# Keeping two pairs of features on chip between gate/up and down, with store slots instead of a staging buffer

## The chip, the cores and the metric

The kernel runs on one core of one Trainium2 chip. Five engines work beside each other and wait for each other by semaphores: PE (matmuls into PSUM; the profile lists its weight loads as PEld), ACT and DVE (elementwise work, both reach PSUM and SBUF), POOL (elementwise work in SBUF) and SP, which here issues nearly all DMAs between HBM and SBUF. The metric is the device time of one execution in microseconds (us).

## What is computed

One layer of a hybrid decoder: three token mixers (dilated attention, a convolution module, sliding-window attention), an output projection with a residual, and a SwiGLU feed-forward block. There are 512 tokens, a model width of 2048 and a feed-forward width of 5632, all in float32. The change touches only the feed-forward block, the last two lines:

```python
def reference(x, norm1_g, w_in, ..., norm2_g, w_gate, w_up, w_down):
    for l in range(DEPTH):                      # DEPTH = 1
        h = _rms_norm(x, norm1_g[l])
        proj = h @ w_in[l]
        ...                                     # three mixers
        mix = jnp.concatenate([out_a, out_b, out_c], axis=-1)
        x = x + mix @ w_out[l]
        h2 = _rms_norm(x, norm2_g[l])
        x = x + (jax.nn.silu(h2 @ w_gate[l]) * (h2 @ w_up[l])) @ w_down[l]
    return x
```

## The kernel before

**Numbers and operands.** PE multiplies numbers of a shortened float32 form, so every operand is split into a high part (rounded) and a low part (what is left). A product is then high x high + high x low + low x high. Moving operands are tiles of 128 x 512: the left 256 columns hold the high part, the right 256 the low part of the same 256 tokens. A matmul with the weights' high part `wh` runs over all 512 columns, one with the low part `wl` over the left 256 and adds into the right half of the PSUM bank; the halves of the bank are added when DVE reads it out (`multiply`, L907 to L916).

**Seven products instead of eight.** The three matrix products of the feed-forward block are done on 2 x 2 blocks: output channels in halves, inputs in halves, tokens in halves. Seven products of sums of blocks, numbered 1 to 7 and taken in the order `ORDER` = 5, 1, 7, 6, 2, 4, 3, give all four output blocks. One such product is called a unit here, seven units a block of the loop at the end (L1071).

**Gate and up.** The 44 tiles of 128 features are taken as 22 pairs p = 0 to 21 (feature tiles p and p + 22). For each pair there is one block for gate and one for up (`Wide`), 44 blocks in all. Their moving operands are the 56 tiles `ops[q, j]` (7 products, 8 inputs j), which stay in SBUF until the last of these blocks. After the up block of a pair its two result tiles `l` and `r` are made into the seven operands that down needs, by POOL's sums `sums1` and `sums2` and by four calls of `piece` at fixed distances behind the block (`later(n, piece, ...)`). `piece` copies its source into PSUM in shortened form (`near`, ACT, L994), copies it again into the high columns of a staging tile (ACT, L995), subtracts to get the low columns (DVE, L996), and queues a store of the tile to the HBM tensor `od` of that pair. A staging tile has 1024 columns, that is two operands, and there are two of them. Three pieces hold two operands (512 KB), the last one holds one (256 KB). `LAID` says in which order the seven operands lie in `od`.

**Down.** 24 blocks (`Down`, `DOWN`) follow, in three rounds over 8 pairs of output tiles. Block t multiplies the operands of pairs `first` to `end - 1`: block d0 those of pairs 0 to 5, d1 0 to 6, d2 1 to 7, and so on with a window of seven that moves by one. Pairs 22 to 27 in this count are pairs 0 to 5 again, in the third round. `load_act(q, pairs)` loads operand q of the given pairs from `od` into slots. During the last gate/up block it is queued after each unit for pairs 0 to 5, 42 loads of 256 KB in all; during block t for the pairs that block t + 1 adds. Tiles with names `a` are these loaded operands.

**Weights.** Each block needs seven weight tiles: four come from HBM ('21', '22', '11', '12'), three are sums made by POOL ('s' in three states, '21' plus '11'; `group`, L160 to L185). `pump` (L204) lets SP issue the next weight loads when a raw buffer is free. `split_up_to` runs two units ahead: ACT makes `wn` in PSUM (L226) and `wh` in SBUF (L227), DVE makes `wl` (L228); three buffers each of `wh` and `wl`.

**Order of work and buffers.** Nothing reorders at run time: every engine goes through its instructions, and SP through its DMAs, in the order in which the program was written out, so a late instruction holds up all behind it on its engine. Work that is not to hold up the units is queued in `evacs` and `extras` and written out one unit at a time. SBUF tiles of 128 x 512 come from one pool of `N_SLOTS` = 71 slots; a tile is given the slot of an earlier one that is done, and its first writer waits for that tile's last reader.

Of the kernel before, what the change touches and what calls it, by code (L numbers as in the profile page):

```python
# [9 lines left out]
F32 = mybir.dt.float32  # L10
F32R = mybir.dt.float32r
# [4 lines left out]
P = 128  # L16
T = 512
# [26 lines left out]
        "bg3 ak2 cq4 ak0 av0 cq6 aq0 ak1 av1 aq1 av2 aq2 ak3 av3 aq3").split()  # L44
ROWS = "c0 c1 c2 c4 c5 c3 c7 c6 a0 a1 b2 b1 b0 b3 a2 a3".split()

N_SLOTS = 71

RAW_PLAIN = "22b sb 21 22a 11 sa 12".split()
RAW_BUFS = 7  # L50
# [12 lines left out]
TH = T // 2  # L63
NJ = KT // 2
NP = NF // 2


_A = [0, 0, 1, 2, 3, 4, 5, 6]
_B = [_A[n] + (6 if n == 0 else 7) for n in range(8)]
_C = [b + 8 for b in _B]  # L70
DOWN = [(n, *w) for ab in (zip(_A, _B), zip(_B, _C), zip(_C, [a + NP for a in _A])) for n, w in enumerate(ab)]

LAID = (5, 7, 6, 4, 3, 1, 2)
# [36 lines left out]
def kernel(ctx: ExitStack, tc: tile.TileContext, xT, wi, wo, wgu, wd, cst_in, outT):  # L110
    nc = tc.nc
    cp = ctx.enter_context(tc.tile_pool(name="consts", bufs=1))
    wp = ctx.enter_context(tc.tile_pool(name="weights", bufs=1))
    sp = ctx.enter_context(tc.tile_pool(name="slots", bufs=N_SLOTS))
    ctx.enter_context(tc.manual_schedule())
# [14 lines left out]
    def slot(name, dt=F32, cols=T):  # L130
        return sp.tile([P, cols], dt, name=name, tag="s")

    def bank(name, cols=T):
        return psum["banks"].tile([P, cols], F32, name=name, tag="b")
# [26 lines left out]
    def group(name, m, n, blocks):  # L161

        key = {k: (k, name) for k in ("11", "12", "21", "22", "s")}
        for k in ("21", "22", "11", "12"):
            entries.append((k + "ab"[m] if k == "22" else k, key[k], blocks[k]))
        u = len(works)

        def add(to, a, b, last=None):
            def go():
                if to == a:  # L170
                    out = raws[key[to]][0]
                else:
                    out = take("s" + "ab"[m], key[to], n)
                nc.gpsimd.tensor_add(out[:, :n], raws[key[a]][0][:, :n], raws[key[b]][0][:, :n])  # L174
                if last:
                    drop(key[last])
            return go

        sums[u - 4].append(add("s", "21", "22"))
        sums[u - 3].append(add("21", "21", "11"))  # L180
        sums[u].append(add("s", "s", "11", "11"))
        sums[u + 2].append(add("s", "s", "12"))
        works.extend((key[k], last, None) for k, last in (
            ("s", False), ("11", False), ("21", True), ("s", False), ("12", True), ("22", True), ("s", True)))

    for p in range(NP):
        for m in range(2):
            group(f"{'gu'[m]}{p}", m, 1024, {f"{i + 1}{k + 1}": [wgu[4 * (p + i * NP) + 2 * m + k]]
                                             for i in range(2) for k in range(2)})

    def down_block(n, half, first, end):

        parts = [(first, min(end, NP)), (0, end - NP)] if first < NP else [(first - NP, end - NP)]
        return [bass.AP(tensor=wd.tensor, offset=wd.offset + (n * P * NF + half * NP + a) * P,
                        ap=[[NF * P, P], [1, (b - a) * P]]) for a, b in parts if b > a]
# [6 lines left out]
    at = {"entry": 0, "split": 0, "use": 0}  # L202
# [29 lines left out]
    def sums_now():  # L232
        for fn in sums.pop(at["use"], ()):
            fn()

    def next_unit():
        sums_now()
        u = at["use"]
        at["use"] += 1
        split_up_to(u + SPLIT_AHEAD)  # L240
        pump(RAW_EARLY if u < 20 else RAW_BUFS)
        return splits.pop(u)
# [119 lines left out]
    for k in range(KT):  # L362
# [9 lines left out]
        hi, lo = h_hl.pop(k)  # L372
# [14 lines left out]
    def project(name):  # L387
        b = bank(name)
        for half in range(2):
            wh, wl = next_unit()  # L390
            for kk in range(8):
                k = 8 * half + kk
                s = slice(kk * P, (kk + 1) * P)
                mm3(b, wh[:, s], wl[:, s], h_hi[k], h_lo[k], k == 0, k == KT - 1)
                if kk % 2 == 1:
                    ticks.tick()
        return b
# [356 lines left out]
    for name in PROJ[HEAD4:]:  # L754
        kind, what, j = name[0], name[1], name[2:]
# [3 lines left out]
        b = project(name)  # L759
# [19 lines left out]
    b = box = boxes = shared = None  # L779
# [60 lines left out]
    for half in range(2):  # L840
        for i, n in enumerate(OUT_ORDER[half]):
            if half == 1 and i == 2:
                ticks.drain()
                b = None
                open_banks(banks=4, high=2)
            b = bank(f"o{half}_{n}")
            wh, wl = next_unit()
            for kk in range(8):
                k = 8 * half + kk
# [4 lines left out]
                s = slice(kk * P, (kk + 1) * P)  # L854
# [20 lines left out]
    def norm2a():  # L875
        n2["r"] = token_scale(ssum2, D, "n2", outs[3][:, :NT])[1]

    def norm2b():
        b = spread(n2["r"], "r2s", outs[3])
        nc.scalar.copy(R_12, b)  # L880
        nc.scalar.copy(r2b[:, T:], b[:, :TH])  # L881

    od = {p: tc.dram_tile([P, 7 * T], F32, name=f"od{p}") for p in range(NP)}
    evacs, extras = [], []
    flip = [1]

    def run(queue):

        for fn, *args in queue.pop(0) if queue else ():
            fn(*args)  # L890

    def later(n, fn, *args, queue=evacs):
        while len(queue) <= n:
            queue.append([])
        queue[n].append((fn, *args))
# [36 lines left out]
    class Wide(Block):  # L932
# [54 lines left out]

        def piece(self, at, src):
            n = src.shape[-1] // TH
            both = wp.tile([P, 2 * T], F32R, name=f"{self.name}st{at}", tag="stage", bufs=2)  # L990
            near = psum["high"].tile([P, 1024], F32R, name=f"{self.name}n{at}", tag="h")[:, :n * TH]
            hi, lo = (both[:, :n * T].rearrange("p (a b c) -> p a b c", a=n, b=2)[:, :, b] for b in range(2))
            src2, near2 = (t.rearrange("p (a b) -> p a b", a=n) for t in (src, near))
            nc.scalar.copy(near, src)  # L994
            nc.scalar.copy(hi, src2)  # L995
            nc.vector.tensor_sub(lo, src2, near2.bitcast(F32))  # L996
            later(0, nc.sync.dma_start, od[self.p][:, at * T:(at + n) * T], both[:, :n * T].bitcast(F32), queue=extras)

        def piece1(self):
            self.piece(0, self.ta)  # L1000
# [15 lines left out]
    def load_y(t):  # L1016
        if t < len(DOWN):
            for n in (DOWN[t][0], DOWN[t][0] + 8):
                y[t, n] = slot(f"y{t}_{n}")
                nc.sync.dma_start(y[t, n], x2d[n])  # L1020
# [37 lines left out]
                self.add(q, t[:, cols])  # L1058
                self.store(n, t, cols)

    acts = {}

    def load_act(q, pairs):
        for j in pairs:
            acts[q, j] = slot(f"a{q}_{j}", F32R)
            at = LAID.index(q)
            nc.sync.dma_start(acts[q, j].bitcast(F32), od[j % NP][:, at * T:(at + 1) * T])
# [3 lines left out]
    for g in range(2 * NP + len(DOWN)):  # L1071
        t = g - 2 * NP
        if t < 0:
            p, m = divmod(g, 2)
            blk = Wide(p, m, gate if m else None)
            gate = blk if m == 0 else None
        else:
            n, first, end = DOWN[t]
            blk = Down(t)
        early_w = []  # L1080
        for i, q in enumerate(ORDER):
            sums_now()
            run(evacs)
            w = next_unit()
            if g == 0 and i < 2:
                blk.multiply(q, w, [ops[q, j] for j in range(EARLY)], last=False)
                early_w.append((q, w))
                if i == 1:
                    for q, w in early_w:
                        blk.multiply(q, w, [ops[q, j] for j in range(EARLY, NJ)], EARLY)  # L1090
                    norm2a()
            elif t < 0:
                blk.multiply(q, w, [ops[q, j] for j in range(NJ)])
            else:
                blk.multiply(q, w, [acts[q, j] for j in range(first, end)])
            if g == 0 and i == 2:
                norm2b()

            if t == -1:
                for j in range(NJ):  # L1100
                    ops.pop((q, j))
                later(1, load_act, q, range(*DOWN[0][1:]), queue=extras)
            elif 0 <= t < len(DOWN) - 1:
                for j in range(first, DOWN[t + 1][1]):
                    acts.pop((q, j))
                later(1, load_act, q, range(end, DOWN[t + 1][2]), queue=extras)
            if t >= -1 and i == 3:
                load_y(t + 1)
            run(extras)
# [85 lines left out]
```

## Time and profile before

| | |
|---|---|
| time, median of 3 runs | 1935.17 us (1934.69 to 1935.21) |
| the profiled execution's own time | 1935.7 us |
| its span, first to last instruction | 1933.9 us |
| mean granted PE clock | 0.992 of full speed |
| PE busy | 1902.3 us (98%), 10332 matmuls |
| DVE busy | 1471.1 us (76%) |
| ACT busy | 1329.0 us (69%) |
| POOL busy | 994.1 us (51%) |
| HBM read, written | 259.09 MB, 57.15 MB |

Times in rows of the profile are microseconds from the start of the span. In rows of a timeline the first number is the start, the second the length; `x6` means six instructions merged in one row; `[0.29 <-DMA a<-od]` says that the engine stood idle for 0.29 us before, and that the end of a load of an `a` tile from `od` ended that. `L916` is line 916 of the kernel. `SPq` is SP's queue: its rows give when a DMA was issued, not when it landed. Names in rows leave out tile numbers: `u21st` is a staging tile of the up block of pair 21, `w('22', 'd1')` the raw weight tile '22' of the down block d1. Busy PE time includes time in which a matmul stands in the pipeline and waits for its operand.

### The profile page before, as it was taken

What the parts mean: (1) busy time and instruction counts of PE and PEld (TensorE: products, weight loads), DVE (VectorE), ACT (ScalarE), POOL (GpSimd) and SP (SyncE); (2) the same over time, 40 slices, a digit from 0 to 9 for tenths busy, and PEclk for the clock granted to TensorE, in tenths of its full rate; (3) what the DMA queues carried; (4) which work ended last, traced back from release to release, by engine and by line L of the source; (5) the groups of instructions that cost most, each with busy time, mean ns of one, the idle gap of its engine ahead of it and who ended that gap; (6) DMA issues with size and microseconds to landing.
All of it is one profiled execution on the core that took longest, in us unless ns stands there. A gap on an engine that the chain in (4) does not pass through costs nothing.

```text
span 1933.9 us, 29230 instructions
## 1 busy us (share of the span) xinstructions
PE 1902.3 (98%) x10332; PEld 1645.4 (85%) x10332; DVE 1471.1 (76%) x2508; ACT 1329.0 (69%) x1782; POOL 994.1 (51%) x640
## 2 busy tenths in 40 slices
PE   8999999999999999999999999999999999999999
PEld 7888888778877888888888888888888788888888
DVE  6789998997468677777777777777777677767776
ACT  6355654553356888888888888888877577667675
POOL 0111011000001788877887888788876566656564
PEclk9999999989999999999999999999999899999999
DMA  7222222223342344444443544354538987777685
GB/s 263 80 100 67 66 89 75 72 86 115 120 127 80 120 158 165 147 148 169 154 157 135 181 141 171 127 181 145 172 128 294 363 277 277 269 242 272 202 278 194
DMA packets 125651, 319.48 MB, mean 165 GB/s; under 512 B 14016, under 2 KB 29504, under 8 KB 125504
## 3 DMA queue, kind: packets, MB, share of 16 engines
q1 hardware_dynamic: 125360, 317.51, 48.0%
q8 instruction: 81, 1.33, 0.3%
q14 instruction: 66, 0.54, 0.1%
q10 hardware_dynamic: 144, 0.10, 0.0%
HBM read 259.09 MB, written 57.15 MB: 164 GB/s over the span
## 4 chain that ended last, share of the span: by engine, by line
PE 69%; DVE 2%; DMA 1%; ACT 1%; issue 0%; DVEq 0%; SPq 0%; ACTq 0%
PE out L916 66%; PE o L246 1%; PE o L245 1%; DMA a<-od 1%; PE o L247 1%; DVE h L802 0%; DMA od<-u21st 0%; DVE xr L826 0%; DVE wl L223 0%; DVE ssum L344 0%; DVE ta L813 0%; ACT sr L343 0%; ACT h L808 0%; DVE wl L228 0%; ACT wh L222 0%
## 5 line engine op out<-in xcount | busy, mean ns | idle before, releaser
L916 PE MATMUL out<-h,wh 128*128 128x512 f32 x2464 | 590.7, 392 | 3.6 <-DVE h L802 3.6
L916 PEld LDWEIGHTS out<-h,wh 128*128 128x128 f32 x2464 | 454.1, 189 | 91.8 <-DVE h L802 4.1
L916 PEld LDWEIGHTS out<-h,wl 128*128 128x128 f32 x2464 | 316.6, 191 | 13.7 <-ACT r2b L881 1.2
L916 PE MATMUL out<-h,wl 128*128 128x256 f32 x2464 | 320.7, 283 | 1.2 <-ACT r2b L881 1.0
L916 PE MATMUL out<-a,wh 128*128 128x512 f32 x1232 | 300.0, 394 | 3.2 <-DMA a<-od 2.6
L916 PEld LDWEIGHTS out<-a,wh 128*128 128x128 f32 x1232 | 226.9, 189 | 50.5 <-DMA a<-od 3.7
L916 PEld LDWEIGHTS out<-a,wl 128*128 128x128 f32 x1232 | 160.9, 193 | 10.9 <-DMA a<-od 4.4
L916 PE MATMUL out<-a,wl 128*128 128x256 f32 x1232 | 164.8, 285 | 2.4 <-DMA a<-od 2.2
L222 ACT CAST wh<-w 128x1024 fp32r<-128x1024 f32 (+1 forms) x93 | 96.8, 1041 | 98.8 <-PE o L246 33.6
L223 DVE TENSOR_TENSOR wl<-w,wh 128x1024 fp32r<-128x1024 f32 (+1 forms) x93 | 112.5, 1210 | 63.9 <-ACT wh L222 63.6
L929 DVE TENSOR_TENSOR y<-y,out 128x256 f32<-128x256 f32 x120 | 50.6, 421 | 65.5 <-PE out L916 62.4
L422 DVE SCALAR_TENSOR_TENSOR y<-bu,cst,y 128x511 f32<-128x511 f32 (+14 forms) x120 | 87.6, 730 | 0.7
L174 POOL TENSOR_TENSOR w('s', 'g0')_5639<-w('21', 'g0')_5403,w('22', 'g0')_5439 128x1024 f32<-128x1024 f32 x1 | 2.4, 2403 | 116.2 <-DVE wl L223 116.2
L930 DVE TENSOR_TENSOR y<-y,out 128x256 f32<-128x256 f32 x120 | 50.5, 421 | 4.1
L246 PE MATMUL o<-ml_c,wh 128*128 128x512 f32 x128 | 51.0, 399 | 2.2 <-DVE ml_c L733 2.2
L245 PE MATMUL cq<-hh,wh 128*128 128x512 f32 x128 | 51.4, 401 | 1.4 <-DVE mix_c L701 1.4
L245 PE MATMUL o<-mh_c,wh 128*128 128x512 f32 x128 | 52.0, 407 | 0.0
L247 PE MATMUL o<-mh_c,wl 128*128 128x512 f32 x128 | 50.8, 397 | 0.0
L247 PE MATMUL cq<-hh,wl 128*128 128x512 f32 x128 | 50.0, 391 | 0.0
L246 PE MATMUL cq<-hl,wh 128*128 128x512 f32 x128 | 49.9, 390 | 0.0
L245 PE MATMUL in<-hh,wh 128*128 128x512 f32 x64 | 26.1, 408 | 5.2 <-ACT wh L222 5.2
L246 PEld LDWEIGHTS o<-ml_c,wh 128*128 128x128 f32 x128 | 24.6, 192 | 7.3 <-DVE ml_c L733 2.9
(3093 smaller groups left out, 4822.5 us busy)
## 6 DMA issues: line engine op xcount, KB each, us to landing
a<-od SPq DMA_DIRECT2D x196, 256.0 KB, 5.3
w<-in_wi SPq DMA_DIRECT2D x59, 512.0 KB, 3.6
w<-in_wo SPq DMA_DIRECT2D x32, 512.0 KB, 3.6
y<-x2d SPq DMA_DIRECT2D x48, 256.0 KB, 5.4
x2d<-y SPq DMA_DIRECT2D x64, 128.0 KB, 3.4
x<-in_xT SPq DMA_DIRECT2D x16, 256.0 KB, 7.2
xr<-in_xT SPq DMA_DIRECT2D x16, 256.0 KB, 3.9
x2d<-xr SPq DMA_DIRECT2D x16, 256.0 KB, 4.1
```

The costliest lines, as they stand in the source:

```text
L174: nc.gpsimd.tensor_add(out[:, :n], raws[key[a]][0][:, :n], raws[key[b]][0][:, :n])
L222: nc.scalar.copy(hi[:, :n], t[:, :n])
L223: eng.tensor_sub(lo[:, :n], t[:, :n], hi[:, :n].bitcast(F32))
L245: nc.tensor.matmul(out, wh, xh, start=start, stop=False)
L246: nc.tensor.matmul(out, wh, xl, start=False, stop=False)
L247: nc.tensor.matmul(out, wl, xh, start=False, stop=stop)
L422: nc.vector.scalar_tensor_tensor(yconv[j][:, i:], hconv[j][:, :T - i], c, yconv[j][:, i:], op0=ALU.mult, op1=ALU.add)
L916: nc.tensor.matmul(out, lhs[:, s], rhs, start=begin, stop=last and low == flip[0] and x is xs[-1], skip_group_check=True)
L929: sign(out, out if first is None else first, main)
L930: sign(out, out, rest)
```

## The change

- `GU_ORDER`: gate and up take the pairs in the order 1 to 5, 7 to 21, 0, 6. The weight groups follow the same order.
- `STAY = (0, 6)`: the seven operands of these two pairs are entered in `acts` as they are made, and `load_act` leaves them out. Pair 6 is not stored to HBM at all. Pair 0 is stored too, since down takes it again in its third round (as pair 22), from HBM.
- `piece` no longer has a staging tile. Each operand gets a slot of its own: one copy into PSUM for the piece as before, then for each of its one or two operands a copy of 256 columns (ACT), a subtraction of 256 columns (DVE) and a store of 256 KB. This holds for all pairs.
- The pool of slots has 75 instead of 71; the four slots take the room of the two staging tiles.

```diff
-N_SLOTS = 71
+N_SLOTS = 75
...
+GU_ORDER = [*range(1, 6), *range(7, NP), 0, 6]
+STAY = (0, 6)
...
-    for p in range(NP):
+    for p in GU_ORDER:
         for m in range(2):
             group(f"{'gu'[m]}{p}", m, 1024, ...)
...
+    acts = {}
...
         def piece(self, at, src):
             n = src.shape[-1] // TH
-            both = wp.tile([P, 2 * T], F32R, name=f"{self.name}st{at}", tag="stage", bufs=2)
             near = psum["high"].tile([P, 1024], F32R, name=f"{self.name}n{at}", tag="h")[:, :n * TH]
-            hi, lo = (both[:, :n * T].rearrange("p (a b c) -> p a b c", a=n, b=2)[:, :, b] for b in range(2))
-            src2, near2 = (t.rearrange("p (a b) -> p a b", a=n) for t in (src, near))
             nc.scalar.copy(near, src)
-            nc.scalar.copy(hi, src2)
-            nc.vector.tensor_sub(lo, src2, near2.bitcast(F32))
-            later(0, nc.sync.dma_start, od[self.p][:, at * T:(at + n) * T], both[:, :n * T].bitcast(F32), queue=extras)
+            for k in range(n):
+                q, s = LAID[at + k], slice(k * TH, (k + 1) * TH)
+                t = slot(f"a{q}_{self.p}", F32R)
+                nc.scalar.copy(t[:, :TH], src[:, s])
+                nc.vector.tensor_sub(t[:, TH:], src[:, s], near[:, s].bitcast(F32))
+                if self.p in STAY:
+                    acts[q, self.p] = t
+                if self.p != STAY[1]:
+                    later(0, nc.sync.dma_start, od[self.p][:, (at + k) * T:(at + k + 1) * T], t.bitcast(F32),
+                          queue=extras)
...
     def load_act(q, pairs):
         for j in pairs:
+            if (q, j) in acts or j == STAY[1]:
+                continue
...
-            p, m = divmod(g, 2)
+            p, m = GU_ORDER[g // 2], g % 2
```

More of the change, by code (lines that the diff above doesn't have):

```diff
@@ L1059, in done @@
                 self.store(n, t, cols)
-    acts = {}
     def load_act(q, pairs):
         for j in pairs:
+            if (q, j) in acts or j == STAY[1]:
+                continue
             acts[q, j] = slot(f"a{q}_{j}", F32R)
```

## The prediction

> **What bounds the kernel now.** I read the page first, then the chain of waits in order of time, then the timelines of PE, SP, POOL and ACT around the one place after 638 us where that chain leaves PE.
>
> ```profile
> span 1933.9 us, 29230 instructions
> ```
> ```profile
> 638.14 853.62 PE out L916 x4906
> 1491.76 5.35 DMA a<-od
> ...
> 1509.32 6.41 DMA od<-u21st
> ...
> 1518.10 412.02 PE out L916 x2366
> ```
> (Columns: start, length, what.) PE sets the end. Gate and up are one unbroken PE stretch, and so is down from 1518.10. Between them lie 26 us in which the chain runs over loads of `a` from `od`, a store of `u21st` and ACT. The change adds and removes no matmul; it can win only there, and can lose anywhere.
>
> ```profile
> 1001.02 3.82 PE L916 MATMUL out<-h,wh 128*128 128x512 f32 x16
> ...
> 1006.59 3.82 PE L916 MATMUL out<-h,wh 128*128 128x512 f32 x16
> ```
> ```profile
> 1487.16 1.52 PE L916 MATMUL out<-a,wh 128*128 128x512 f32 x6
> ...
> 1495.81 0.38 PE L916 MATMUL out<-a,wl 128*128 128x256 f32 x1 [0.29 <-DMA a<-od]
> 1496.48 0.39 PE L916 MATMUL out<-a,wl 128*128 128x256 f32 x1 [0.30 <-DMA a<-od]
> ...
> 1504.55 0.39 PE L916 MATMUL out<-a,wl 128*128 128x256 f32 x1 [0.29 <-DMA a<-od]
> ```
> Undisturbed, one wh and one wl matmul together take (1006.59-1001.02)/16 = 0.348 us, and a unit of eight such pairs 2.79. Down's first block d0 starts at 1487.16; by 1518.10 d0 (7 units of 6) and the first unit of d1 (7) are done: 49 x 0.348 = 17.05 us of work in 30.94. The handover costs 13.9 us, much more than PE's marked waits.
>
> In it single matmuls start 0.67 us apart (1495.81, 1496.48), each with its own load of 256 KB: the DMA engines are full.
>
> ```profile
> 1430.00:1450.00 20.00, 20.00 (x112) 17.45 (x111) 14.44 (x20) 15.22 (x18) 14.66 (x9) 1.00 0.37 119
> 1480.00:1490.00 10.00, 10.00 (x59) 8.83 (x58) 6.47 (x10) 5.66 (x8) 5.38 (x5) 1.00 1.05 388
> 1505.00:1506.00 1.00, 1.00 (x5) 0.86 (x4) 0.00 (x0) 0.00 (x0) 0.00 (x0) 0.86 0.99 390
> 1515.00:1516.00 1.00, 1.00 (x5) 0.90 (x5) 0.18 (x1) 0.60 (x2) 1.00 (x1) 0.52 1.06 399
> ```
> (By stretch: length, busy PE, PEld, DVE, ACT and POOL, granted clock, DMA share, GB/s.) At 388 GB/s, 256 KB take 0.675 us. Behind those loads, in SP's order, come d1's weights:
>
> ```profile
> L1067 SPq DMA_DIRECT2D a<-od x36: 319/320/470, 1471.3 to 1499.5; - x36
> ```
> ```profile
> 1500.50 0.33 SPq L209 DMA_DIRECT2D w('22', 'd1')_14819<-in_wd  x1
> ```
> ```profile
> 1506.92 2.07 POOL L174 TENSOR_TENSOR w('s', 'd1')_14902<-w('21', 'd1')_14817,w('22', 'd1')_14819 128x896 f32<-128x896 f32 x1 [13.93 <-DMA w('22', 'd1')_14819<-in_wd]
> ...
> 1514.00 0.73 POOL L986 TENSOR_TENSOR u21tb<-u21tb,u21l 128x256 f32<-128x256 f32 x1
> ```
> ```profile
> 1514.76 0.59 ACT L994 CAST u21n<-u21tb 128x512 fp32r<-128x512 f32 x1 [3.96 <-POOL u21tb L986]
> 1515.75 0.62 ACT L995 CAST u21st<-u21tb 128x512 fp32r<-128x512 f32 x1 [0.40 <-DMA od<-u21st]
> 1516.28 0.90 ACT L226 CAST wn<-w('11', 'd1')_14821 128x896 fp32r<-128x896 f32 x1
> ...
> 1521.32 0.37 ACT L994 CAST u21n<-u21l 128x256 fp32r<-128x256 f32 x1
> 1521.62 0.40 ACT L995 CAST u21st<-u21l 128x256 fp32r<-128x256 f32 x1
> 1521.93 0.90 ACT L226 CAST wn<-w('12', 'd1')_14885 128x896 fp32r<-128x896 f32 x1
> ```
> This is what ends last. POOL waits 13.93 us for w22 of d1, then does seven sums in a row (two of weights, three of y, two of the last pair's pieces), and the copies of that piece stand ahead of the split of w11 on ACT. PE gets its wh at 1518.10, 11.18 us after w22 has landed. That PE is also slowed by single loads of `a` is hidden under this chain.
>
> **The change part by part.**
>
> *Fewer loads at the handover.* Pair 0 stays on chip, so d0 loads five pairs for each of 7 operands. Ahead of d1's w22 on SP stand 30 loads instead of the 36 of the row above: 6 x 0.675 = 4.05 us. Upper end: those 36 start within 28.2 us, 0.81 each with what lies between, 4.8 us. Lower end: if SP idles around the first twelve, only four loads count, 2.7 us. I take 4.05, the rate of the engines, because their share is 1.05 while this goes on. w22 lands at 1506.92-4.05 = 1502.87.
>
> *POOL's seven sums.* Same number, same order: from w22's landing to ACT's start 1514.76-1506.92 = 7.84 us. ACT begins the piece at 1510.71.
>
> *The last pair's pieces.* The last pair is now 6. It isn't stored, so the wait of 0.40 us for a stage buffer goes. One copy of 512 columns (1515.75 to 1516.28, 0.53 us from start to start) becomes two of 256 (1521.32, 1521.62, 1521.93: 0.30 and 0.31): +0.08. From 1514.76 to 1518.10 were 3.34 us; now 3.02. PE starts d1's second unit at 1510.71+3.02 = 1513.73, 4.37 us earlier.
>
> *Is PE there in time?* The last load of a4 (1504.55; six loads before it gone) comes at 1500.5, the last of a3 (below; seven gone) at 1507.3. Then one wh and six wl matmuls (two thirds and one third of 0.348) end d0 at 1508.3, and d1's first unit, 7 x 0.348, ends at 1510.7; at half clock, 4.9 us, near 1513.9. Either way PE waits for ACT or is just about there: `a` still isn't last.
>
> ```profile
> 1512.02 0.29 PEld L916 LDWEIGHTS out<-a,wh 128*128 128x128 f32 x1 [0.38 <-DMA a<-od]
> ```
>
> *Seven loads of pair 6 for d1 and the last pair's stores* also go: 14 x 0.675 = 9.5 us of DMA work. In SP's order they lie behind w11 of d1, and PE waits for nothing after it (the unbroken 412.02 us), so I count nothing. They would matter if d2's weights became late.
>
> *Pieces of all pairs.* For each pair ACT gets 11 copies instead of 8, DVE 7 subtractions instead of 4, SP 7 stores instead of 4. In each of three pieces ACT's busy time grows by 2 x 0.40 - 0.62 = 0.18 and DVE's by 2 x 0.422 - 0.686 = 0.16. I take nothing on the path: the lead of the weight splits covers it.
>
> ```profile
> 1025.38 1.05 ACT L227 CAST wh<-w('12', 'g10')_9785 128x1024 fp32r<-128x1024 f32 x1 [0.51 <-PE out L916]
> ```
> ```profile
> L996 DVE TENSOR_TENSOR u21st<-u21tb,u21n x1: 686/686/686, 1515.8 to 1515.8; 128x512 fp32r<-128x512 f32 x1
> L996 DVE TENSOR_TENSOR u21st<-u21l,u21n x1: 422/422/422, 1521.7 to 1521.7; 128x256 fp32r<-128x256 f32 x1
> ```
> ```profile
> 1029.61 1.21 DVE L228 TENSOR_TENSOR wl<-w('22', 'g10')_9727,wn 128x1024 fp32r<-128x1024 f32 x1
> ```
> With three split buffers, the wh whose buffer PE released at 1025.38 is used two units later, at 1030.95, and the next one (w22) at 1033.7; its wl is done at 1030.82. This lead of 2.9 us is the shortest I found over a pair, and a piece eats 0.34 of it. Without that cover the price is 22 x 3 x 0.34 = 22 us. Three more issues of 0.32 us per pair on SP hide behind its own waits for split buffers (row below); the stores run at a DMA share of 0.37.
>
> ```profile
> SPq L209 <- DVE wl L228: 668.0, 132, 14.6
> ```
>
> [...]
>
> *Order of pairs, 75 slots, two pairs held.* The same work in another order; ahead of gate and up only slot addresses differ. At the handover pieces and loads wait for slots that PE left a block earlier: nothing, or 0.5 us either way.
>
> Sum: the profiled run's 1935.7 (span 1933.9 and 1.8 around it) less 4.37 is 1931.3. The median of the runs, 1935.17, is 0.53 below the profiled run, so **1930.8 us**, 0.23% less.
>
> **The rivals.**
> 1. *The clock drops where PE waits.* It is 0.86 at 1505 and 0.52 at 1515, and ACT's lateness hid that. Now PE may idle up to three us ahead of 1513.73; if the gate falls there, the work after it runs at half speed until the clock comes back. Before, that took from the last load (1512.02) to the half of the row of 1515, 3.5 us: +1.7, so 1932.5. Against it: the clock will fall in the waits for a3 already and be back when the idle time comes.
>    [...]
> 2. *Something else than those loads holds w22*, a slot or a split: no change, 1935.2. The share of 1.05 speaks against it.
> 3. *All 13.9 us go*: 1921.3. That needs the chain of 11 us ready when an undisturbed d0 ends, 1487.16 + 42 x 0.348 = 1501.8, before w22 has even landed.
> 4. *Slower:* the added copies and subtractions delay a wl in each pair. It decides once a piece costs 2.9 us instead of 0.34, as when DVE stands behind both ACT copies of a late piece; then PE waits in every pair, up to 22 us, 1957. In 853 us of unbroken PE nothing speaks for it.
>
> **How the numbers follow.** Forecast 0.66, rivals 0.15, 0.08, 0.05 and 0.06. The forecast's own ends are gains of 3.0 us (2.7 + 0.3) and 5.1 (4.8 + 0.3): 1930.1 to 1932.2; with the clock on top 1933.9; with 0.5 of slot effects, 1929.5 to 1934.3. Rivals 2, 3 and 4 (0.19) stay outside. A change of 0.2%, 3.87 us, is about what a measurement of this kernel can tell from none; 3/4 of the forecast lies beyond it. Faster 0.54, same 0.40, slower 0.06.
>
> **What would show it.** Right: POOL's sum of d1's w21 and w22 starts near 1502.9, PE's unbroken stretch of down near 1513.7, gate and up stay one stretch of 853.6 us, the last ACT pieces wait for no DMA. Wrong: a PE wait in gate and up; a clock below 1 after 1514; w22 landing at 1506 or later; d2's weights late.

## The result, and the profile after

The changed kernel takes 1932.25 us (median of 22 runs, 1930.64 to 1935.04), the kernel before, measured beside it, 1935.22 (22 runs, 1934.14 to 1937.06). The ratio is 0.9987, with a 95% interval from 0.9981 to 0.9993: 2.97 us faster, where 4.37 were forecast. The profiled execution of the changed kernel took 1934.18 us, with a span of 1932.4. In the code of the changed kernel, lines behind the new constants are 4 or more further down: L916 of before is L921 here.

The chain of waits after the change (start, length, what):

```profile
641.10 853.06 PE out L921 x4903
...
1499.47 6.29 DMA w('22', 'd1')_15059<-in_wd
1505.84 1.12 POOL w('s', 'd1')_15138 L178
...
1515.66 0.94 ACT wh L231
1516.64 412.02 PE out L921 x2366
```

PE's timeline at the handover after the change (start, length, and in brackets the wait before and what ended it):

```profile
1490.12 1.52 PE L921 MATMUL out<-a,wh 128*128 128x512 f32 x6
...
1507.64 0.50 PE L921 MATMUL out<-a,wh 128*128 128x512 f32 x1 [2.08 <-DMA a<-od]
...
1516.64 1.89 PE L921 MATMUL out<-a,wh 128*128 128x512 f32 x7 [1.25 <-ACT wh L231]
```

POOL's and ACT's timelines there:

```profile
1505.84 2.07 POOL L178 TENSOR_TENSOR w('s', 'd1')_15138<-w('21', 'd1')_15057,w('22', 'd1')_15059 128x896 f32<-128x896 f32 x1 [9.86 <-DMA w('22', 'd1')_15059<-in_wd]
```
```profile
1513.68 0.59 ACT L996 CAST u6n<-u6tb 128x512 fp32r<-128x512 f32 x1 [3.96 <-POOL u6tb L991]
1514.20 0.71 ACT L1000 CAST a<-u6tb 128x256 fp32r<-128x256 f32 x2
1514.82 0.90 ACT L230 CAST wn<-w('11', 'd1')_15061 128x896 fp32r<-128x896 f32 x1
```

In what follows the handover is the time from d0's first matmul to the first of d1's second unit, 49 pairs of matmuls. It went from 30.94 us (1487.16 to 1518.10) to 26.52 (1490.12 to 1516.64): 4.42 us less. From there to the end, PE needs 412.02 us in both; gate and up, from their first matmul to d0's, 849.02 in both (638.14 to 1487.16, 641.10 to 1490.12). But gate and up begin at 641.10 instead of 638.14. The front of the kernel, where the change was to alter nothing but slot addresses, is 2.96 us longer in this execution. So two things were to be tested: which part of the change shortened the handover, and what lengthened the front.

PE's timeline near 225 us, of the kernel before and of the changed one, is where most of the difference begins:

```profile
225.45 0.39 PE L688 MATMUL c2o<-c2pl,cv 128*128 128x256 f32 x1 [1.67 <-DVE c2pl L674]
```
```profile
226.88 0.58 PE L692 MATMUL c2o<-c2pl,cv 128*128 128x256 f32 x1 [2.64 <-DVE c2pl L678]
```

ACT's timeline there, before and after:

```profile
215.67 1.28 ACT L409 ACT_TABLE_LOAD   x1
222.33 0.63 ACT L409 ACTIVATE bg<-bg 128x512 f32<-128x512 f32 x1 [5.37 <-DVE bg L408]
```
```profile
222.82 1.28 ACT L413 ACT_TABLE_LOAD   x1 [6.64 <-DVE bg L412]
224.12 0.63 ACT L413 ACTIVATE bg<-bg 128x512 f32<-128x512 f32 x1
```

Before, ACT loaded its table for the sigmoid of `bg3` at 215.67, while it had nothing else to do, and then waited for DVE. After, it waits first, and the 1.28 us of the load lie behind the wait. The compiled order of ACT says why: with 75 slots `bg3` gets the slot of `bg2`, which POOL read last, so the sigmoid has a second wait, and the wait for DVE becomes an instruction of its own ahead of the table load. When the changed kernel is compiled with 71 slots, the order of before comes back.

```
before   LoadActFuncSet
         Activation bg<-bg   [waits DVE]
after    EventSemaphore      [waits DVE]
         LoadActFuncSet
         Activation bg<-bg   [waits Pool]
```

From ACT the delay reaches PE by way of POOL and DVE. POOL multiplies by the sigmoid's result (`bu<-bu,bg`) as soon as it is there. Rows of POOL and DVE, before and after:

```profile
223.12 1.53 POOL L412 TENSOR_TENSOR bu<-bu,bg 128x512 f32<-128x512 f32 x1 [5.55 <-ACT bg L409]
224.49 0.18 DVE L621 SCALAR_TENSOR_TENSOR c7d<-c7d,cq7r 128x2 f32<-128x2 f32 x1
```
```profile
224.82 1.26 POOL L416 TENSOR_TENSOR bu<-bu,bg 128x512 f32<-128x512 f32 x1 [6.77 <-ACT bg L413]
224.94 1.17 DVE L625 SCALAR_TENSOR_TENSOR c7d<-c7d,cq7r 128x2 f32<-128x2 f32 x1
```

After, a small operation of DVE begins 0.12 us behind POOL's multiplication, takes 1.17 us instead of 0.18, and ends 0.03 us behind it. In the compiled program it waits neither for ACT nor for POOL. A table load of ACT (224.76 to 226.04) lies beside it as well, but the first operation of `y` (L424), which begins at 63.41 beside another of these multiplications and no table load, also takes 1.50 us where it mostly takes 0.54. The `c2pl` for which PE waits comes two operations later on DVE.

In these two profiles nearly all of the 2.96 us can be placed. 0.45 us are there before DVE makes `bg` (221.61 and 222.06); where they come from stays open. The wait for `c2pl` is 0.97 longer. From the matmul behind that wait to the next one of `c7s` (L611, 227.94, and L615, 230.87) PE needs 3.99 us instead of 2.49 for the same matmuls: 1.50 us, in a stretch in which the granted clock was lower (0.68 from 226 to 228 and 0.50 from 228 to 230, against 1.00 in both stretches of the kernel before; wider windows in the last experiment below).

### The profile page after: what moved, and what is told of

Its sections match the earlier page's. It is cut to its first block, busy times and chain, and to the rows that moved or that the text cites. A ratio compares the mean times of both kernels' runs of the same rounds, so it can differ in the third digit from the quotient of the medians.

```text
span 1932.4 us, 29509 instructions
## 1 busy us (share of the span) xinstructions
PE 1899.8 (98%) x10332; PEld 1645.2 (85%) x10332; DVE 1474.8 (76%) x2574; ACT 1334.0 (69%) x1848; POOL 993.4 (51%) x640
## 4 chain that ended last, share of the span: by engine, by line
PE 70%; DMA 1%; DVE 0%; POOL 0%; ACT 0%; issue 0%; POOLq 0%; DVEq 0%
PE out L921 66%; PE o L250 1%; PE o L249 1%; PE o L251 1%; DMA w('22', 'd1')_15059<-in_wd 0%; DMA a<-od 0%; POOL w('21', 'd1')_15057 L178 0%; DVE xr L830 0%; PE out L289 0%; DVE h L806 0%; ACT sr L347 0%; ACT h L812 0%; DVE wl L232 0%; POOL w('s', 'd1')_15138 L178 0%; ACT wh L231 0%
## 5 line engine op out<-in xcount | busy, mean ns | idle before, releaser
L921 PE MATMUL out<-h,wh 128*128 128x512 f32 x2464 | 591.0, 392 | 3.6 <-DVE h L806 3.6
L921 PEld LDWEIGHTS out<-h,wh 128*128 128x128 f32 x2464 | 454.1, 189 | 91.8 <-DVE h L806 4.0
L921 PEld LDWEIGHTS out<-h,wl 128*128 128x128 f32 x2464 | 317.5, 192 | 13.8 <-ACT r2b L885 1.2
L921 PE MATMUL out<-h,wl 128*128 128x256 f32 x2464 | 321.5, 283 | 1.2 <-ACT r2b L885 0.9
L921 PE MATMUL out<-a,wh 128*128 128x512 f32 x1232 | 297.8, 392 | 4.2 <-DMA a<-od 3.0
L921 PEld LDWEIGHTS out<-a,wh 128*128 128x128 f32 x1232 | 226.0, 188 | 50.1 <-DMA a<-od 5.3
L921 PEld LDWEIGHTS out<-a,wl 128*128 128x128 f32 x1232 | 160.4, 193 | 8.1 <-DMA a<-od 1.5
L921 PE MATMUL out<-a,wl 128*128 128x256 f32 x1232 | 163.0, 284 | 0.9 <-DMA a<-od 0.9
```

Source lines behind the costliest of these rows:

```text
L921: nc.tensor.matmul(out, lhs[:, s], rhs, start=begin, stop=last and low == flip[0] and x is xs[-1], skip_group_check=True)
```

## The experiments

**The table load first.** In the changed kernel:

```diff
         nc.vector.tensor_mul(t, bg, r1b)
+        if j == 3:
+            nc.scalar.activation(early, nhalf[:, :1], AF.Sigmoid)
         nc.scalar.activation(t, t, AF.Sigmoid)
```

> The changed kernel with one tiny sigmoid on a constant in front of the third glu activation (bg3), so that ACT loads its table before it waits for DVE, as in the kernel before. Theory (the other slot addresses gave that activation a second wait, which pushed the wait for DVE in front of the table load; 1.28 us of table load are then no longer hidden, and the idle PE loses its clock now and then): the wait of PE for c2pl near 225 us is 1.7 us again instead of 2.6, gate and up begin near 639, the handover stays at 26.5, and the time is 1930.8 (1932.25 less some 1.4). Rival (the front differs only by chance, by where the clock falls): 1932.2, with runs between 1930.6 and 1935.0 as in the changed kernel.

1930.26 us, ratio to before 0.9976 (0.9967 to 0.9985), with 1934.97 for before beside it. PE's rows, from its timeline and the chain:

```profile
225.43 0.38 PE L694 MATMUL c2o<-c2pl,cv 128*128 128x256 f32 x1 [1.65 <-DVE c2pl L680]
```
```profile
637.99 853.08 PE out L923 x4903
...
1513.59 412.02 PE out L923 x2366
```

The wait is 1.65 again, gate and up begin at 637.99, and the handover is 26.58 (its first matmul of d0 starts at 1487.01). The difference to before is 4.71 us instead of 2.97: by the medians, 1.74 us had been lost to the late table load. The 11 runs lie between 1928.8 and 1931.09, about half as wide as the 22 of the changed kernel. All further experiments but the next one and the repeat of the changed kernel contain this edit.

**The kernel before, with its table load late.**

```diff
         nc.vector.tensor_mul(t, bg, r1b)
+        if j == 3:
+            nc.scalar.copy(early, t[:, :1])
         nc.scalar.activation(t, t, AF.Sigmoid)
```

> The kernel before, with one copy of a single column of bg3 by ACT ahead of its sigmoid, so that the wait for DVE stands in front of the table load, as in the changed kernel. Nothing else differs. Theory (that order of wait and table load is what the front of the changed kernel lost): PE waits some 2.7 us for c2pl near 226 us instead of 1.67, and the time is 1936.0 to 1937.5 (1.0 of wait, and up to 1.4 in those runs in which the clock drops there). Rival (the lost front was chance): 1935.0, and 1.7 us of wait or a little more for the added copy.

1936.37 us against 1935.20, ratio 1.0008 (0.9999 to 1.0016). ACT and PE:

```profile
221.98 0.19 ACT L410 COPY early<-bg 128x1 f32<-128x1 f32 x1 [6.66 <-DVE bg L408]
222.19 1.28 ACT L411 ACT_TABLE_LOAD   x1
```
```profile
225.99 0.39 PE L690 MATMUL c2o<-c2pl,cv 128*128 128x256 f32 x1 [2.56 <-DVE c2pl L676]
```

The same wait appears in the old kernel, and 1.17 us with it, at the low end of what was expected. The interval still holds no change at all, so the size is not shown by this run alone. But the wait comes with the late table load and goes with the early one, in both kernels, and DVE is held beside POOL here too (224.34 to 225.48 beside 224.19 to 225.45): that is the cause of the longer wait. Its price in the median is some 1.2 to 1.7 us.

**Only the slots and smaller pieces, nothing kept.**

```diff
-GU_ORDER = [*range(1, 6), *range(7, NP), 0, 6]
-STAY = (0, 6)
+GU_ORDER = [*range(NP)]
+STAY = (-1, -1)
```

> As the kernel of the table experiment, but no pair is kept and the pairs go in order 0 to 21: only the slots of their own for each operand, with the smaller copies and stores, are left of the change. Theory (36 loads stand ahead of the weight tile 22 of d1 again): handover 30.6 instead of 30.94, no wait in gate and up, time 1934.9. Rival 1 (the smaller pieces and stores are what helped): handover 26.5, 1930.8. Rival 2 (the added copies cost time in gate and up): above 1936.

**Only pair 0 kept.**

```diff
+GU_ORDER = [*range(1, NP - 1), 0, NP - 1]
+STAY = (0, -1)
```

> As the kernel of the table experiment, but only pair 0 is kept, and the order is 1 to 20, 0, 21, so that pair 21 is last and is stored as before. Theory (30 instead of 36 loads ahead of the weight tile 22 of d1): handover 26.6, 1930.9. Rival (the loads and stores of pair 6 that went are what helped): handover 30.6, 1934.9.

**Only pair 6 kept.**

```diff
+GU_ORDER = [*range(6), *range(7, NP), 6]
+STAY = (-1, 6)
```

> As the kernel of the table experiment, but only pair 6 is kept, in the order 0 to 5, 7 to 21, 6; d0 loads six pairs again. Theory (36 loads ahead of the weight tile 22 of d1): handover 30.6, 1934.8. Rival (the loads and stores of pair 6 that went are what helped): handover 26.5, 1930.8.

Measured: slots alone 1933.87 us, ratio 0.9996 (0.9987 to 1.0005); pair 0 alone 1929.86, 0.9975 (0.9965 to 0.9985); pair 6 alone 1933.96, 0.9995 (0.9986 to 1.0004). For each, in this order, PE's first matmul of d0 and POOL's sum of w21 and w22 of d1 (timelines), and PE's last unbroken stretch (chain):

```profile
1486.26 1.52 PE L923 MATMUL out<-a,wh 128*128 128x512 f32 x6
...
1505.43 2.07 POOL L178 TENSOR_TENSOR w('s', 'd1')_15159<-w('21', 'd1')_15070,w('22', 'd1')_15072 128x896 f32<-128x896 f32 x1 [13.32 <-DMA w('22', 'd1')_15072<-in_wd]
...
1516.22 412.19 PE out L923 x2366
```
```profile
1485.61 1.52 PE L923 MATMUL out<-a,wh 128*128 128x512 f32 x6
...
1500.85 2.07 POOL L178 TENSOR_TENSOR w('s', 'd1')_15145<-w('21', 'd1')_15058,w('22', 'd1')_15060 128x896 f32<-128x896 f32 x1 [9.38 <-DMA w('22', 'd1')_15060<-in_wd]
...
1511.64 412.02 PE out L923 x2366
```
```profile
1486.31 1.52 PE L923 MATMUL out<-a,wh 128*128 128x512 f32 x6
...
1505.80 2.07 POOL L178 TENSOR_TENSOR w('s', 'd1')_15153<-w('21', 'd1')_15070,w('22', 'd1')_15072 128x896 f32<-128x896 f32 x1 [13.64 <-DMA w('22', 'd1')_15072<-in_wd]
...
1516.60 412.02 PE out L923 x2366
```

From d0's start, w22 is summed after 19.17, 15.24 and 19.49 us, and the handovers are 29.96, 26.03 and 30.29. Only with pair 0 kept does w22 come earlier. So pair 0, six loads less ahead of d1's weights, is nearly the whole gain, 3.9 us of the handover and 4.0 of the median against the slots alone. The slots alone also shortened the handover, by 0.98 us where 0.34 was expected; their 1.1 us in the median lie within the interval of no change. Keeping pair 6 gives nothing that can be measured, and the smaller pieces cost nothing that can be measured.

**The piece of the last pair one unit later.** In the changed kernel ACT is last, since it makes a piece of pair 6 ahead of the split of w11 (rows of ACT above: piece at 1513.68, split at 1514.82).

```diff
-                                     (5, self.piece2), (8, self.piece4)):
+                                     (6 if self.p == GU_ORDER[-1] else 5, self.piece2), (8, self.piece4)):
```

> The kernel of the table experiment, with the second piece of the last pair (6) one unit later, so that ACT splits w11 of d1 ahead of it. Theory (in the changed kernel PE waits 1.25 us for that split after the first unit of d1, and nothing else): handover 25.3 instead of 26.58, 1929.0. Rival (something else takes the place, the loads of a or the clock): handover 26.6, 1930.3.

1928.47 us, ratio 0.9967 (0.9955 to 0.9979). PE's timeline:

```profile
1486.70 1.52 PE L923 MATMUL out<-a,wh 128*128 128x512 f32 x6
...
1509.56 3.36 PE L923 MATMUL out<-a,wh 128*128 128x512 f32 x14
1512.76 1.83 PE L923 MATMUL out<-a,wl 128*128 128x256 f32 x14
```

The 14 matmuls at 1509.56 are seven of d1's first unit and seven of its second, in one run with no wait between; the second starts half of 3.20 us later, at 1511.16. The handover is 24.46, 2.1 us less than with the table experiment alone; 1.28 were expected. The 1.25 us of wait behind that figure were read from the changed kernel; in the profile of the table experiment PE waited only 0.23 us there, at 1513.59. The clock was 0.58 from 1505 to 1510 and 0.73 from 1510 to 1515 in that profile, so PE was hardly ahead of ACT. Here it was 0.66 from 1505 to 1510 and 1.00 from 1510 on. So the 2.1 us took both, ACT out of the way and the clock back earlier; why it came back earlier stays open, and what the order on ACT is worth alone isn't shown. The interval of the ratio also overlaps that of the table experiment.

**Loads before the last block.** SP and the DMA engines have a gap between the last stores of pair 0 and the weights of d0, as the windows of the changed kernel show (length; busy PE, PEld, DVE, ACT, POOL; granted clock, DMA share, GB/s):

```profile
1465.00:1470.00 5.00, 5.00 (x29) 4.35 (x29) 4.25 (x8) 5.00 (x9) 4.18 (x5) 1.00 0.35 128
1470.00:1475.00 5.00, 5.00 (x30) 4.41 (x29) 2.47 (x5) 3.75 (x6) 4.26 (x3) 1.00 0.20 41
```

On top of the later piece, five loads (a5 for pairs 1 to 5) go into that gap, the loads of the other operands but a3 move one unit forward:

```diff
+            if t == -2 and i == 6:
+                later(0, load_act, ORDER[0], range(*DOWN[0][1:]), queue=extras)
             if t == -1:
...
-                later(1, load_act, q, range(*DOWN[0][1:]), queue=extras)
+                if i != 5:
+                    later(1, load_act, ORDER[min(i + 1, 6)], range(*DOWN[0][1:]), queue=extras)
```

> The kernel of the later piece, with the five loads of a5 for d0 queued before the last gate/up block instead of inside it, and those of a1, a7, a6, a2 and a4 one unit earlier. SP and the DMA engines are idle between 1468 and 1473 and the slots are free. Theory (from 1474 to 1510 the DMA engines are what is short, so 5 loads of 0.675 us taken out of that stretch move w22 of d1 and the last loads of a3 forward by 3.4 us): handover 21.9, 1925.6. Rival (the loads come no earlier than the slots that gate and up leave): handover 25.3, 1929.0.

And ten loads, with a1 too and the others two units forward:

```diff
+            if t == -2 and i >= 5:
+                later(0, load_act, ORDER[i - 5], range(*DOWN[0][1:]), queue=extras)
...
-                later(1, load_act, q, range(*DOWN[0][1:]), queue=extras)
+                if i < 4:
+                    later(1, load_act, ORDER[i + 2], range(*DOWN[0][1:]), queue=extras)
+                elif i == 6:
+                    later(1, load_act, q, range(*DOWN[0][1:]), queue=extras)
```

> As the kernel with five loads early, but ten: a5 and a1 before the last gate/up block, the others two units earlier. Theory (6.75 us of DMA work taken out of the full stretch): w22 of d1 lands some 6.75 us earlier, d0 runs almost without waits, handover 17.5 to 19, 1921.5 to 1923. Rival (SP stands at a load whose slot isn't free yet, and the weights of d0 behind it come late): PE waits at the end of gate and up, 1926 to 1931.

Five: 1924.57 us, ratio 0.9946 (0.9932 to 0.9959). Ten: 1921.98 us (1920.14 to 1922.78), ratio 0.9931 (0.9918 to 0.9943). PE's and POOL's timelines and the windows of the second:

```profile
1486.75 1.52 PE L923 MATMUL out<-a,wh 128*128 128x512 f32 x6
...
1502.21 3.36 PE L923 MATMUL out<-a,wh 128*128 128x512 f32 x14
...
1506.96 1.09 PE L923 MATMUL out<-a,wl 128*128 128x256 f32 x7 [0.56 <-DVE wl L232]
```
```profile
1495.75 2.15 POOL L178 TENSOR_TENSOR w('s', 'd1')_15139<-w('21', 'd1')_15058,w('22', 'd1')_15060 128x896 f32<-128x896 f32 x1 [3.15 <-DMA w('22', 'd1')_15060<-in_wd]
```
```profile
1465.00:1470.00 5.00, 5.00 (x31) 4.47 (x30) 3.73 (x6) 3.76 (x5) 4.77 (x3) 1.00 1.02 359
1470.00:1475.00 5.00, 5.00 (x31) 4.43 (x31) 3.39 (x4) 5.00 (x8) 3.51 (x2) 1.00 1.00 359
```

The gap is filled, w22 of d1 is summed 9.00 us after d0's start instead of 15.72, and PE runs through d0 without a wait. The second unit of d1 starts half of the 14 matmuls (1.60 us) after 1502.21, at 1503.81, a handover of 17.06 us, a little below what was expected; with five loads early it was 20.43 (1485.52 to 1505.95), 1.5 less than expected. The work itself takes 17.05, so all 13.9 us are gone; what is left is 0.56 us for one `wl`. This version is 13.2 us faster than the kernel before and 10.3 faster than the changed one.

**The same with no pair kept.**

```diff
-GU_ORDER = [*range(1, 6), *range(7, NP), 0, 6]
-STAY = (0, 6)
+GU_ORDER = [*range(NP)]
+STAY = (-1, -1)
```

> The kernel with ten loads early, but no pair is kept and the pairs go in order 0 to 21, so that d0 loads six pairs and twelve loads come early. Theory (what counts is how many loads the full stretch still holds; 24 instead of 20 stand ahead of w22 of d1, 2.7 us, and six instead of five of a3 behind it): handover 20 to 21.5, 1924.9 to 1926.4, far ahead of the changed kernel with no pair kept. Rival (early loads only help because the kept pairs leave room on the queue and in the slots): 1930 or more.

1928.39 us, ratio 0.9963 (0.9948 to 0.9977). PE, POOL and a window:

```profile
1486.98 1.52 PE L923 MATMUL out<-a,wh 128*128 128x512 f32 x6
...
1502.75 4.06 PE L923 MATMUL out<-a,wh 128*128 128x512 f32 x6 [2.45 <-DMA a<-od]
```
```profile
1500.93 2.07 POOL L178 TENSOR_TENSOR w('s', 'd1')_15159<-w('21', 'd1')_15070,w('22', 'd1')_15072 128x896 f32<-128x896 f32 x1 [8.11 <-DMA w('22', 'd1')_15072<-in_wd]
```
```profile
1505.00:1510.00 5.00, 5.00 (x18) 4.08 (x18) 2.51 (x6) 2.72 (x6) 4.92 (x7) 0.50 1.05 397
```

The expectation missed by 2 us and more, and the rival isn't right either. w22 is summed 13.95 us after d0's start. With two pairs kept and ten loads early it was 9.00, so the difference is 4.95 us. The expectation counted four loads more in the full stretch, 2.7 us. All six would make 4.05, and that fits better, since with the loads forward the DMA share is already 0.95 from 1465 to 1470; what the rest is stays open. After a wait of 2.45 us PE then ran at half clock from 1505 to 1510. Early loads and the later piece help without any pair kept (about 5.5 us against the slots alone), and the kept pairs give another 6.4 on top.

**The changed kernel once more.**

> The changed kernel once more, unchanged, for a second profile of it. Its times lie in two groups, near 1931.5 and near 1934. Theory (the later table load costs 1.0 us always, and in some executions the clock drops in the longer wait as well): the wait for c2pl is 2.6 us again; in an execution of the first group the clock stays at 1.00 from 220 to 230 and gate and up begin near 639, in one of the second group it drops there and they begin near 641; the handover is 26.5 in both. Rival (the groups come from the handover): the front is the same in both groups and the handover differs by 2.5.

1931.9 us, ratio 0.9984 (0.9975 to 0.9994). The profiled execution took 1933.70. Windows of it, of the first profile after the change and of before:

```profile
220.00:230.00 10.00, 7.02 (x32) 5.73 (x32) 8.50 (x19) 7.24 (x15) 1.26 (x1) 0.83 0.17 52
```
```profile
220.00:230.00 10.00, 7.03 (x32) 5.77 (x31) 8.50 (x19) 7.11 (x15) 1.26 (x1) 0.84 0.15 52
```
```profile
220.00:230.00 10.00, 7.89 (x46) 6.45 (x45) 8.78 (x23) 6.96 (x16) 1.53 (x1) 1.00 0.17 54
```

Both profiles of the changed kernel come from the longer of its executions, and both show a clock drop after the long wait for `c2pl`, which the profile of before doesn't have. The handover is 26.34 (1489.83 to 1516.17) in this one. No execution near 1931.5 was caught with a profile, so it stays open whether that clock is what separates the two groups of times. That the spread halves with the table load put right speaks for it; the 1.50 us found above for the lower clock are less than the 2.5 between the groups.

## Why the prediction was right, and where it was off

The time, 1932.25, is 1.45 us above the forecast of 1930.8. It lies in the wide range, 1929.5 to 1934.3, but 0.05 above the 1932.2 at which the forecast's own terms end. The wide range allows for the clock and for slots at the handover. Nothing was lost there; the loss came in the front, for which the sum had no term. So the mechanism of the gain was right, and it is luck that the allowance was wide enough for a loss elsewhere. The signs named show the same: w22 was to be summed near 1502.9 and down's stretch to begin near 1513.7; they came at 1505.84 and 1516.64, both 2.9 us late, because d0 began at 1490.12 instead of 1487.16.

*Fewer loads at the handover.* Right. 4.05 us were forecast for w22; in the changed kernel it is summed 15.72 us after d0's start instead of 19.76, 4.04 earlier. That it fits to a hundredth is chance: among the profiles with six pairs loaded the time is 19.76, 19.17 and 19.49, among those with five 15.72, 15.78 and 15.24. The experiments with one pair each show that pair 0's loads are the cause.

*POOL's seven sums.* 7.84 us from w22 to ACT's start was carried over; 1513.68 - 1505.84 is 7.84.

*The last pair's pieces.* 3.02 us were forecast from ACT's start to PE's; 1516.64 - 1513.68 is 2.96. With this the handover's 4.37 came out at 4.42.

*Is PE there in time?* Right: PE waited for ACT, 1.25 us, and `a` was not last. "Just about there" was right as well: in the table experiment, with the clock at 0.58 from 1505 to 1510 (1.00 in the changed kernel), the wait was 0.23.

*Pair 6, the pieces of all pairs.* Nothing was counted, and nothing was found (ratios 0.9995 and 0.9996). The price of a piece in busy time was overestimated: two copies take 0.71 us together where one took 0.62, 0.09 more and not 0.18. In 700 us of gate and up, before and after:

```profile
700.00:1400.00 700.00, 700.00 (x4022) 618.52 (x4022) 523.76 (x720) 574.59 (x683) 559.70 (x360) 1.00 0.45 155
```
```profile
700.00:1400.00 700.00, 700.00 (x4028) 618.72 (x4027) 527.31 (x774) 578.76 (x737) 559.84 (x360) 1.00 0.45 156
```

DVE is busy 3.55 us longer, ACT 4.17, and PE is full in both.

*Order of pairs, 75 slots, two pairs held.* Here the forecast failed. It said that "ahead of gate and up only slot addresses differ", and gave 0.5 us either way at the handover and nothing in the front. An address is not all that a slot brings: its last user comes with it as a wait. One such wait put a table load behind another wait, which cost 1.2 us (put into the kernel before) to 1.7 (taken out of the changed one). 4.4 less 1.2 to 1.7 are the 3 us that were measured; without it the changed kernel takes 1930.26. The wait doesn't stand where the text above the prediction puts it, at the first writer of the slot (DVE), but at the second, the sigmoid.

*The rivals.* The first rival's 1932.5 is nearer to the measured time than the forecast, but what it describes did not happen. What it calls the gate shows in the kernel before as a granted clock of 0.50 from 1506 to 1516 and of 1.00 from 1516 to 1518. In the changed kernel the clock did drop, to 0.53 between 1510 and 1512, and was back at 1.00 by 1514, as the forecast argued: the drop came in the waits for a3, and ACT's lateness covered it. The clock that did cost time fell near 227 us (0.68 from 226 to 228), where no rival looked. The loads did hold w22. All 13.9 us went in an experiment, but it took the piece moved and ten loads early besides the kept pairs; "ready when an undisturbed d0 ends" was the right condition, and it can be met. The pieces did not eat the lead of the splits.

```profile
1510.00:1512.00 2.00, 1.80 (x7) 1.55 (x7) 0.00 (x0) 0.00 (x0) 2.00 (x4) 0.53 0.46 161
...
1514.00:1516.00 2.00, 1.40 (x7) 0.82 (x5) 1.67 (x5) 2.00 (x5) 1.72 (x1) 1.00 0.00 0
```

## What to carry to other kernels

A stage that was short of DMA time (share 1.05) was shortened by the loads that left it: six loads not made took 3.9 us off the handover, five and ten moved into an idle stretch just ahead 4.0 and 7.4. So look for the gap in the queue when you think of paying with on-chip room. Here both together gave the most. A new number of buffers can bring new waits in every stage that uses the pool, also in those that the change doesn't touch, so compare the waits of the compiled program and not only the order of its instructions; here one of them cost 1.2 to 1.7 us. Where a table load was hidden in an idle time, a tiny activation of the same function ahead of the wait kept it there: the load began at 215.75 instead of 222.82, and PE's wait was 1.65 us instead of 2.64.

## What the runs showed of the hardware that was not expected

- A wait of an activation stood ahead of the table load in front of it: in the changed kernel ACT began the load at 222.82, behind a wait of 6.64 us for DVE; in the kernel before it began it at 215.67, ahead of a wait of 5.37. The load takes 1.28 us, and the activation behind it began 0.02 us after its end (222.82 + 1.28 = 224.10, 224.12).
- DVE was held beside POOL without a wait in the program: an operation on 128x2 numbers took 1.17 us instead of 0.18 and ended 0.03 us behind POOL's multiplication, which had begun 0.12 us before it. The repeat of the changed kernel (224.80 to 225.96 beside 224.69 to 225.95) and the kernel before with its late table load show the same. In the kernel before, beside POOL's multiplication at 223.12, DVE's operations were not held (0.43 us for `c7s`, 0.14 for its readout), and the multiplication took 1.53 us instead of 1.26; what decides between the two isn't shown.
- A wait of 2.64 us on PE was followed by a lower clock in the profile of the changed kernel (0.84 from 220 to 230), one of 2.65 in its repeat as well (0.83), one of 2.56 in the kernel before with its late table load was not (1.00): its first matmul behind the wait took 0.39 us, not 0.58. What decides it isn't shown.
- 256 KB loads, with some weight tiles among them, still moved 359 to 397 GB/s where they filled the DMA engines (share 1.00 to 1.05, windows of the experiments with early loads).
